# An attention block's transposes moved ahead of its value products, and a 96-row gate operand padded to 128 rows

## The chip, the core and the metric

The kernel runs on one core of a Trainium2 chip. Its time is device microseconds (us) of one execution, and what is compared is the median of several runs. The core has five engines with an instruction queue each: PE (TensorE, matrix products; PEld is its weight load), DVE (VectorE), ACT (ScalarE), POOL (GpSimd) and SP (SyncE, which here issues the DMA transfers). The order of each engine's instructions is fixed when the program is built, and an engine runs its own in that order, waiting wherever an operand or a buffer isn't ready.

## The reference: one step of a two-layer decoder

512 prompt tokens and 32 sample tokens (8 sequences of 4) go through an RWKV-7 layer and then a native sparse attention (NSA) layer, all in float32. Two places matter here.

The gate of the RWKV layer, whose low rank is 160:

```
g = jax.nn.sigmoid(xg @ g1) @ g2          # g1 (1024, 160), g2 (160, 1024)
```

and the attention of the NSA layer, which for each of 4 key heads `k` with 4 query heads each forms three softmaxes (compressed, selected and window keys), each times its values, and adds them with gates:

```
o_c = jnp.einsum('tkgn,nkd->tkgd', p_c.astype(v_cmp.dtype), v_cmp)
o_s = jnp.einsum('tkgjs,tkjsd->tkgd', p_s.astype(vg.dtype), vg)
o_w = jnp.einsum('tkgl,lkd->tkgd', p_w.astype(v_win.dtype), v_win)
o = g[..., 0:1] * o_c + g[..., 1:2] * o_s + g[..., 2:3] * o_w
```

With 512 prompt tokens the window and the selection hold all earlier tokens, so both are plain causal attention.

## The kernel before

`layer0` is the RWKV layer and `layer1` the NSA layer. Dense products are done in three passes of a split of each float32 operand into two `fp32r` parts (`products`, line 326, 128 x 128 weights against 272 tokens). Layer 1 has 28 such dense jobs (`dense`, in the order of `JO`), whose matmuls are mixed in between the attention's as filler: `together(attend(k), mix(jobs, sample), n)` takes `n` steps of the filler for each step of the attention.

Attention goes over key heads `k` = 0 to 3 and, in each, over four blocks `b` of 128 queries in the order `BO[k]`. `scores(k, b)` computes the score products (line 1733: 64 rows of contraction, 128 columns), adds the bias and takes the maximum on DVE (1740), the exponential on ACT (1743), and scales on DVE or POOL (1759). `values(k, b)` of one block runs beside `scores` of the next. It has 2(b+1) steps. Each step transposes the probabilities of four query heads into one PSUM bank (1777), copies them to an SBUF tile `h` on ACT (1780) or DVE (1782) in the pattern `aav`, and multiplies them with the values into `po`: line 1784, two column halves of 128 rows x 64 columns each (`PARS`), which write the lower and the upper 64 partitions. At the end the compressed branch is added into the same `po` (1789), `po` is copied out by ACT (1791), and it goes to DRAM, or in the last head to `gate` (1976) and `split`.

The sample tokens' attention (`attend_sample`) runs as filler as well: score products (1844, 128 rows x 32 columns), ten exponentials on ACT (1869), transposes (1885 to 1890), and value products (1918, 128 rows x 32 columns) on K and V rows that are loaded into tiles `s`. After the last head, `project_out` (326) and `project_last` (2009) multiply with the output weights; 2009 does tokens 256 to 511 (`h` = 1) first, then 0 to 255.

In this text a *form* of a matmul is its rows of contraction x columns of weights, rounded up to 32, 64 or 128: 1733 and 1693 are 64 x 128, 1784 and 1789 are 128 x 64, 1844 and 1918 are 128 x 32, and the dense jobs and the transposes are 128 x 128.

The buffers of layer 1 come from `M1`: 7 tiles `s` (sample rows, and at first the compression weights), 18 tiles `p` (K, V and queries), 6 tiles `h` (transposed probabilities and others). PSUM has 5 banks `pw` for the attention and 3 `ph` for the dense jobs.

In the gate of layer 0 (`gates`), the last 32 of the 160 hidden columns are stacked three times with their split parts into one operand of 96 rows (`gs`, `g2b`), so that one matmul does three products; line 361 (`stacked`) runs these beside the 128-row products. POOL writes rows 64 to 95 of `g2b` (685).

## Time and profile before

| | |
|---|---|
| median of 3 runs | 1086.18 us (1080.42 to 1086.69) |
| the profiled execution | 1075.55 us |
| its span, first to last instruction | 1073.8 us, mean granted TensorE clock 0.963 |
| PE busy | 990.1 us, 92% of the span |
| DVE, ACT, POOL busy | 621.1, 545.3, 454.0 us |
| attention of layer 1, first value transpose to the last | 692.7 to 1060.0 us |

A row of a group view gives the line, engine, operation, operands (`out<-in`, buffer numbers left out) and count, then busy time and mean duration, then the idle time just before these instructions and what ended it. In a timeline, the columns are the start in us, the duration, engine, line, operation and count of a merged run, and in brackets idle time with what ended it. In the view by windows each engine has its busy us, `(x...)` is its number of instructions, and `PEclk` is the granted TensorE clock as a share of full speed.

### The profile page before, as it was taken

The page shows a single profiled execution, that of the slowest core. Times are in us where ns is not written, and L with a number is a line of the kernel's source. Part 1 is how long each engine was busy: PE and PEld are TensorE (multiplying, and loading weights), DVE is VectorE, ACT ScalarE, POOL GpSimd, SP SyncE. Part 2 cuts the span into 40 slices and gives each one's busy share as a digit, 9 for nine tenths or more (in the row PEclk, how much of TensorE's full clock was granted, in tenths as well). Part 3 has the DMA queues.
Part 4 walks back from the last instruction along what each step waited for, and adds up shares of the span by engine and source line. Part 5 has one row for each costly group of instructions (what it writes and reads, how often), then busy time and mean ns, then how long its engine had stood idle before and what let it go on. Part 6 is the DMA issues. An engine that isn't in the chain of part 4 may idle for free.

```text
span 1073.8 us, 24587 instructions
## 1 busy us (share of the span) xinstructions
PE 990.1 (92%) x9525; PEld 838.6 (78%) x9525; DVE 621.1 (58%) x1390; ACT 545.3 (51%) x1254; POOL 454.0 (42%) x516
## 2 busy tenths in 40 slices
PE   5799998989999989999879799999899998998997
PEld 4789997978768678787778798986676774787876
DVE  4787679797666443468658234336555454327455
ACT  4456775646343354455445454456745646455352
POOL 5914647756620643213122757543224262145320
PEclk8799999999999999999989899999899996999999
DMA  5585435548472546635855533323242231327533
GB/s 187 189 277 192 136 118 155 191 154 262 121 209 74 170 129 190 194 96 146 192 177 169 166 110 107 95 79 115 70 136 76 70 105 41 105 84 263 152 114 104
DMA packets 149447, 153.54 MB, mean 143 GB/s; under 512 B 52946, under 2 KB 99570, under 8 KB 149074
## 3 DMA queue, kind: packets, MB, share of 16 engines
q1 hardware_dynamic: 149330, 151.97, 47.3%
q8 instruction: 75, 1.23, 0.5%
q14 instruction: 42, 0.34, 0.1%
HBM read 111.33 MB, written 43.93 MB: 145 GB/s over the span
## 4 chain that ended last, share of the span: by engine, by line
PE 53%; DVE 7%; DMA 6%; issue 4%; POOL 4%; ACT 3%; SPq 1%; DVEq 0%; POOLq 0%; ACTq 0%
PE ph L326 23%; PE pw L1733 5%; PE pw L1784 4%; PE pw L1777 4%; PE pr L1140 2%; DMA d<-dram 1%; PE ph L2009 1%; DMA w<-in_wo 1%; DVE l L288 1%; POOL l L288 1%; DMA tb<-dram 1%; DVE tmp L1042 1%; DVE p L721 1%; PE ph L1270 1%; PE pw L1789 1%
## 5 line engine op out<-in xcount | busy, mean ns | idle before, releaser
L326 PE MATMUL ph<-x,l 128*128 128x272 f32 x2448 | 359.4, 297 | 11.0 <-DVE l L288 3.3
L326 PEld LDWEIGHTS ph<-x,l 128*128 128x128 f32 x2448 | 322.5, 191 | 42.6 <-issue 20.8
L288 POOL TENSOR_TENSOR l<-w,l 128x512 fp32r<-128x512 f32 (+2 forms) x118 | 155.5, 1331 | 218.6 <-ACT l L287 202.2
L287 ACT ACTIVATE l<-w 128x512 fp32r<-128x512 f32 (+2 forms) x160 | 92.9, 613 | 149.7 <-PE ph L326 68.9
L326 PE MATMUL pp<-x,l 128*128 128x272 f32 x768 | 111.4, 299 | 5.9 <-POOL l L288 5.9
L326 PEld LDWEIGHTS pp<-x,l 128*128 128x128 f32 x768 | 103.7, 194 | 8.5 <-POOL l L288 6.2
L1743 ACT ACTIVATE a<-a,st 128x512 f32<-128x512 f32 (+3 forms) x128 | 70.6, 553 | 47.5 <-DVE st L1740 47.3
L1740 DVE CUSTOM_DVE_ANT_0 a<-pw,tb 128x512 f32<-128x512 f32 (+3 forms) x128 | 57.2, 487 | 58.0 <-PE pw L1733 57.6
L1733 PE MATMUL pw<-p,p 64*128 64x512 f32 (+3 forms) x256 | 65.0, 485 | 0.0
L1784 PE MATMUL pw<-h,p 128*64 128x256 f32 x320 | 52.4, 418 | 8.7 <-ACT h L1780 8.7
L1483 DVE TENSOR_TENSOR d<-ph,RS 128x272 f32<-128x272 f32 x56 | 24.3, 437 | 55.3 <-PE ph L326 50.9
L326 PE MATMUL pp<-t,l 128*128 128x272 f32 x384 | 54.2, 293 | 0.0
L1777 PE MATMUL pw<-cst,a 128*128 128x128 f32 x320 | 51.4, 292 | 1.5 <-DVE a L1759 1.5
L1777 PEld LDWEIGHTS pw<-cst,a 128*128 128x128 f32 x320 | 37.3, 147 | 19.4 <-issue 14.5
L1780 ACT ACTIVATE h<-pw 128x512 f32<-128x512 f32 x60 | 35.0, 590 | 32.5 <-PE pw L1777 32.1
L326 PEld LDWEIGHTS pp<-t,l 128*128 128x128 f32 x384 | 50.2, 188 | 0.7
L288 DVE TENSOR_TENSOR l<-w,l 128x512 fp32r<-128x512 f32 x42 | 36.5, 878 | 20.4 <-ACT l L287 20.2
L288 POOL TENSOR_TENSOR d<-d,d 128x544 fp32r<-128x544 f32 (+2 forms) x21 | 28.2, 1343 | 44.2 <-ACT d L287 35.4
L1759 DVE TENSOR_SCALAR a<-a,st 128x128 f32<-128x128 f32 (+3 forms) x112 | 43.4, 447 | 0.9
L1733 PEld LDWEIGHTS pw<-p,p 64*128 64x128 f32 x256 | 27.7, 193 | 18.4 <-issue 12.1
L1784 PEld LDWEIGHTS pw<-h,p 128*64 128x64 f32 x320 | 17.2, 139 | 26.3 <-ACT h L1780 11.0
L657 POOL TENSOR_TENSOR d<-d,d 128x544 f32<-128x544 f32 x8 | 10.8, 1346 | 56.4 <-ACT d L375 54.9
(415 smaller groups left out, 1937.9 us busy)
## 6 DMA issues: line engine op xcount, KB each, us to landing
w<-in_rkvz SPq DMA_DIRECT2D x64, 256.0 KB, 3.0
d<-dram SPq DMA_DIRECT2D x54, 272.0 KB, 4.2
w<-in_win SPq DMA_DIRECT2D x56, 256.0 KB, 3.0
dram<-d SPq DMA_DIRECT2D x48, 272.0 KB, 2.6
ab<-dram SPq DMA_DIRECT2D x32, 256.0 KB, 3.8
p<-in_xT SPq DMA_DIRECT2D x16, 272.0 KB, 3.8
tb<-dram SPq DMA_DIRECT2D x16, 264.0 KB, 4.9
dram<-uar SPq DMA_DIRECT2D x8, 512.0 KB, 3.7
```

The lines of the kernel that those rows point to most:

```text
L287: nc.scalar.activation(hi, raw, AF.Copy)
L288: (eng or nc.gpsimd).tensor_tensor(lo, raw, hi.bitcast(F32), OP.subtract)
L326: nc.tensor.matmul((pt[h][:m, :HN] if split else pt[:m, h, :HN]), a[:, k, :m], b[:, h * HN:(h + 1) * HN], start=(k == 0 and n == 0), stop= ...
L1140: nc.tensor.matmul(pg[par][r, i], BK[r, i, par], AR[r, i].rearrange("p a b -> p (a b)"), start=True, stop=True)
L1483: self.nc.vector.tensor_tensor(o, p, r, OP.mult)
L1733: nc.tensor.matmul(p[par][:, :n], Q[2 * k + m][r, tk], kk[par][r, :n], start=True, stop=True)
L1740: nc.vector.tensor_tensor_reduce(out=P[j], in0=p[par][:, :n], in1=tb, scale=-1.0, scalar=3.0e38, op0=OP.add, op1=OP.min, accum_out=st[:, 0 ...
L1743: nc.scalar.activation(P[j], P[j], AF.Exp, scale=-1.0, bias=st[:, 0, g, j:j + 1], accum_out=st[:, 1, g, j:j + 1])
L1759: (nc.gpsimd if e == "p" else nc.vector).tensor_scalar(pj, pj, rr, None, op0=OP.mult)
L1777: nc.tensor.transpose(pt[:, g % 2, g // 2], PB[g][j][:, c * 128:c * 128 + 128], ident)
L1780: nc.scalar.activation(w, pt, AF.Copy)
L1784: nc.tensor.matmul(po[r], v, w[:, par], start=(x == 0), stop=False, skip_group_check=True)
```

## The change

```diff
@@ PLAN
-    'M1': {'s': 7, 'p': 18, 'tb': 2, 'a': 12, 'h': 6, 'ct': 2, 'sc': 2},
+    'M1': {'s': 6, 'p': 13, 'tb': 2, 'a': 12, 'h': 12, 'ct': 2, 'sc': 2},
@@ gates, in layer 0
             gs = self.stack(self.t("p", dt=F32R), hid, 32)
             nc.scalar.activation(gs[64:96], hid[:32], AF.Copy)
+            nc.gpsimd.memset(gs[96:128].bitcast(F32), 0.0)
...
                 nc.gpsimd.tensor_tensor(g2b[64:96], raw[64:96], g2b[64:96].bitcast(F32), OP.subtract)
+                nc.gpsimd.memset(g2b[96:128].bitcast(F32), 0.0)
...
-                    self.stacked(pt, [(g2[0][:, c], gh), (g2[0][:, c], gl), (g2[1][:, c], gh), (g2b[:96, c], gs[:96])])
+                    self.stacked(pt, [(g2[0][:, c], gh), (g2[0][:, c], gl), (g2[1][:, c], gh), (g2b[:, c], gs)])
@@ values(k, b), in layer 1
             PB = self.PB[k, b]
-            po = self.t("pw", (128, 2, 128))
             steps = [(j, c, V[k][:, c]) for j, V in ((0, VS), (1, VW)) for c in range(b + 1)]
             ns = len(steps)
+            W = []
             for x, (j, c, v) in enumerate(steps):
...
-                for r, par in PARS:
-                    nc.tensor.matmul(po[r], v, w[:, par], start=(x == 0), stop=False, skip_group_check=True)
+                W.append(w)
                 for _ in range((4 * (x + 1)) // ns - (4 * x) // ns):
                     yield
+
+            po = self.t("pw", (128, 2, 128))
             for m in range(2):
                 for r, par in PARS:
-                    nc.tensor.matmul(po[r, m], VM[:, k, 2 * m + par], CT[k][:, b], start=False, stop=True, skip_group_check=True)
+                    nc.tensor.matmul(po[r, m], VM[:, k, 2 * m + par], CT[k][:, b], start=(m == 0), stop=False, skip_group_check=True)
+            for x, (j, c, v) in enumerate(steps):
+                for r, par in PARS:
+                    nc.tensor.matmul(po[r], v, W[x][:, par], start=False, stop=(x == ns - 1), skip_group_check=True)
             ok = self.t("h", (128, 2, 128))
```

The number of instructions of every kind stays the same but for three memsets on POOL. The order of the instructions that comes out of it moves. In the rows below a name like `pw_12648` is one buffer, and `x2` stands for two instructions of one row; lines after the change are 2 to 6 higher than before (transposes 1779 for 1777, value products 1795 for 1784, the compressed part 1792 for 1789, scores 1735 for 1733, copies 1782, 1784 and 1797 for 1780, 1782 and 1791, the sample's exponentials 1875 for 1869).

First place: PE, in the last head, where the value products of a block of eight steps stand (`po` is `pw_12648` before and `pw_12894` after). Before:

```order
L326 MATMUL ph_12695<-x_12251,l_12684 128x272
L1784 MATMUL pw_12648<-h_12663,p_10691 64x256 x2
L326 MATMUL ph_12695<-x_12250,l_12685 128x272
L326 MATMUL ph_12695<-x_12259,l_12684 128x272
L1784 MATMUL pw_12648<-h_12726,p_10691 64x256 x2
L1784 MATMUL pw_12648<-h_12735,p_10691 64x256 x2
L326 MATMUL ph_12695<-x_12260,l_12684 128x272
L326 MATMUL ph_12695<-x_12259,l_12685 128x272
L1733 MATMUL pw_12763<-p_9828,p_10985 128x384
```

After:

```order
L326 MATMUL ph_12880<-x_12244,l_12871 128x272
L1792 MATMUL pw_12894<-ct_12634,VM 64x128 x4
L1795 MATMUL pw_12894<-h_12656,p_10685 64x256 x2
L1795 MATMUL pw_12894<-h_12663,p_10685 64x256 x2
...
L1795 MATMUL pw_12894<-h_12851,p_10812 64x256 x2
L1735 MATMUL pw_12924<-p_9826,p_10906 128x128
```

Before, the block's products stand in seven places between dense matmuls; after, the compressed part and all eight steps stand in one run. Over layer 1, from the first score product on, consecutive matmuls on PE change their form 298 times before and 234 times after, and the products into `po` (1784, 1789) stand in 75 runs before and 31 after; up to that point both orders have the same number of changes.

Second place: PE, in the third head (`k` = 2), right behind the transposes of its compressed branch (1714). Before:

```order
L1733 MATMUL pw_11318<-p_10016,p_10234 128x384
L1777 MATMUL pw_11330<-cst,a_11018 128x128
L1777 MATMUL pw_11330<-cst,a_11057 128x128
L1777 MATMUL pw_11330<-cst,a_11118 128x128
L1777 MATMUL pw_11330<-cst,a_11155 128x128
L1784 MATMUL pw_11329<-h_11335,p_10691 64x256 x2
L1777 MATMUL pw_11339<-cst,a_11018 128x128
...
L1733 MATMUL pw_11451<-p_9827,p_10480 128x384
L1784 MATMUL pw_11329<-h_11344,p_10691 64x256 x2
L1733 MATMUL pw_11452<-p_9828,p_10480 128x384
```

After:

```order
L1735 MATMUL pw_11321<-p_10019,p_10232 128x384
L1779 MATMUL pw_11332<-cst,a_11021 128x128
...
L1779 MATMUL pw_11388<-cst,a_11151 128x128
L1735 MATMUL pw_11445<-p_9825,p_10472 128x384
...
L1735 MATMUL pw_11448<-p_10019,p_10472 128x384
L1779 MATMUL pw_11459<-cst,a_11022 128x128
...
L1779 MATMUL pw_11546<-cst,a_11152 128x128
L1792 MATMUL pw_11580<-ct_11315,VM 64x128 x4
```

Before, the first value product stands right behind the first four transposes. After, two runs of 16 transposes (four steps each) with four score products between them come ahead of the first value product. No dense matmul stands among these rows on either side; the next one follows after 36 rows before and after 66 rows now.

Third place: ACT, in the second head, where the sample's exponentials stand. Before:

```order
L1743 ACTIVATE a_9405,st_9291<-a_9405,st_9291 128x384
L1869 ACTIVATE s_9979,sst_10157<-s_9979,sst_10157 128x256
L1869 ACTIVATE s_10142,sst_10157<-s_10142,sst_10157 128x256
...
L1743 ACTIVATE a_9406,st_9291<-a_9406,st_9291 128x384
L1780 ACTIVATE h_9416<-pw_9411 128x512
```

After:

```order
L1745 ACTIVATE a_9452,st_9294<-a_9452,st_9294 128x384
L1782 ACTIVATE h_9416<-pw_9411 128x512
...
L1782 ACTIVATE h_9537<-pw_9532 128x512
L1875 ACTIVATE s_10153,sst_10157<-s_10153,sst_10157 128x120
...
L1875 ACTIVATE s_10153,sst_10157<-s_10153,sst_10157 128x32 x2
L1745 ACTIVATE a_9615,st_9513<-a_9615,st_9513 128x256 x2
L1782 ACTIVATE h_9625<-pw_9620 128x512
```

Before, eight of the ten exponentials stand ahead of the copy `h_9416` of the first transposed step in this stretch; after, all ten stand behind that copy and two more.

## The prediction

> **What bounds the kernel now.** I read the page from the top: busy shares, the 40 slices, the chain that ended last, then the groups.
>
> ```profile
> PE 990.1 (92%) x9525; PEld 838.6 (78%) x9525; DVE 621.1 (58%) x1390; ACT 545.3 (51%) x1254; POOL 454.0 (42%) x516
> ...
> PEclk8799999999999999999989899999899996999999
> ...
> PE 53%; DVE 7%; DMA 6%; issue 4%; POOL 4%; ACT 3%; SPq 1%; DVEq 0%; POOLq 0%; ACTq 0%
> ...
> L1784 PE MATMUL pw<-h,p 128*64 128x256 f32 x320 | 52.4, 418 | 8.7 <-ACT h L1780 8.7
> ```
>
> PE is busy for 92% of the span and carries over half of the chain; no other engine passes 58%. So time is won only by shortening what PE does, or by taking away one of its few waits. In layer 1 dense matmuls fill the attention's gaps, and the longest waits are the 8.7 us for the copies of 1780. The clock row has a 6 among its nines just there, in slice 34.
>
> A busy PE can still lose time between matmuls. The timeline of PE in the last head shows it, where nothing waits:
>
> ```profile
> 1014.19 1.53 PE L1777 MATMUL pw<-cst,a 128*128 128x128 f32 x12
> 1015.48 2.48 PE L326 MATMUL ph<-x,l 128*128 128x272 f32 x18
> ...
> 1027.46 0.65 PE L1784 MATMUL pw<-h,p 128*64 128x256 f32 x4
> 1028.04 1.52 PE L326 MATMUL ph<-x,l 128*128 128x272 f32 x10
> 1029.49 0.65 PE L1784 MATMUL pw<-h,p 128*64 128x256 f32 x4
> 1030.07 0.39 PE L326 MATMUL ph<-x,l 128*128 128x272 f32 x1
> 1030.39 1.08 PE L1784 MATMUL pw<-h,p 128*64 128x256 f32 x8
> 1031.41 1.27 PE L326 MATMUL ph<-x,l 128*128 128x272 f32 x8
> ```
>
> From start to start, one step's products (x4) hold PE for 0.58 us and two steps' (x8) for 1.02 us, so a step itself is worth 0.44 us, and 0.14 us is paid once per run. A dense run of one takes 0.32 us and one of ten 1.45 us: 0.126 us each, and 0.19 us once per run. Transposes next to dense matmuls, which have the same form, pay nothing of the kind: twelve in 1.29 us, 0.108 us each. So a change of form costs (0.14 + 0.19) / 2 = 0.165 us.
>
> **The change, part by part.**
>
> *Fewer changes of form.* In layer 1 the order has 298 changes before and 234 after, 64 fewer, each on the engine that bounds: 64 x 0.165 = 10.6 us. The saving is smaller than the 44 runs of value products that vanish would suggest (88 changes), since the sample's products (1918, a form of their own) are spread over more runs now. I take 10.5 us, with bounds of 8 (some changes stand beside waits) and 12 (0.19 for each).
>
> *The wait in the second head.* The timeline of PE, and the view by windows:
>
> ```profile
> 752.79 0.65 PE L1784 MATMUL pw<-h,p 128*64 128x256 f32 x4 [2.21 <-ACT h L1780]
> ...
> 755.06 0.33 PE L1777 MATMUL pw<-cst,a 128*128 128x128 f32 x1 [1.18 <-DVE a L1759]
> 755.72 0.48 PE L1777 MATMUL pw<-cst,a 128*128 128x128 f32 x1 [0.33 <-DVE a L1759]
> 757.31 1.12 PE L1784 MATMUL pw<-h,p 128*64 128x256 f32 x4 [1.12 <-ACT h L1780]
> ```
> ```profile
> 755.00:760.00 5.00, 3.49 (x14) 2.19 (x14) 2.98 (x15) 2.74 (x11) 1.56 (x3) 0.56 0.09 26
> 760.00:765.00 5.00, 5.00 (x31) 2.96 (x30) 2.16 (x9) 2.27 (x9) 1.53 (x4) 0.76 0.04 5
> ```
>
> PE stands for 4.84 us in four pieces, and behind that the granted clock is 0.56 and 0.76 over ten microseconds: 5 x 0.44 + 5 x 0.24 = 3.4 us lost, some 0.7 of it while PE stood anyway. Together 7.5 us. The reason is on ACT, where the sample's exponentials run ahead of the copy (here in the third head, the same ten):
>
> ```profile
> 887.81 0.38 ACT L1869 ACTIVATE s<-s,sst 128x120 f32<-128x120 f32 x1
> ...
> 888.19 0.49 ACT L1869 ACTIVATE s<-s,sst 128x256 f32<-128x256 f32 x1
> ...
> 888.68 0.49 ACT L1869 ACTIVATE s<-s,sst 128x256 f32<-128x256 f32 x1
> ...
> 889.17 0.31 ACT L1869 ACTIVATE s<-s,sst 128x32 f32<-128x32 f32 x1
> ...
> 889.47 0.31 ACT L1869 ACTIVATE s<-s,sst 128x32 f32<-128x32 f32 x1
> ```
>
> Start to start they take 0.38 (120 wide), 0.49 (256) and 0.30 us (32); two, four and four of them make 3.9 us. In the new order three copies go ahead of all ten. The first product that needs a copy from behind them comes on PE only after 12 dense matmuls (1.5 us), 22 transposes (2.4), the eight score products and eight value products, some 7 us altogether, against 3.9 us of exponentials and two exponentials of scores. So most of the wait is covered. Waits of the 1759 kind can come back, since the blocks still follow each other. I take 5 us gained; bounds 0 and 7.5.
>
> *The wait in the third head.*
>
> ```profile
> 892.96 1.12 PE L1784 MATMUL pw<-h,p 128*64 128x256 f32 x4 [4.63 <-ACT h L1780]
> 894.02 2.82 PE L1777 MATMUL pw<-cst,a 128*128 128x128 f32 x12
> ```
> ```profile
> 890.00:895.00 5.00, 2.04 (x9) 1.28 (x10) 0.76 (x5) 5.00 (x20) 0.00 (x0) 0.71 0.17 53
> 895.00:900.00 5.00, 5.00 (x16) 2.73 (x15) 3.28 (x10) 2.62 (x6) 3.51 (x4) 0.50 0.16 58
> 900.00:905.00 5.00, 5.00 (x13) 1.44 (x12) 1.04 (x4) 0.69 (x3) 0.91 (x3) 0.50 0.19 53
> 905.00:910.00 5.00, 5.00 (x23) 3.84 (x23) 1.08 (x5) 2.49 (x8) 0.00 (x0) 0.58 0.00 0
> ```
>
> Here 4.63 us of standing are followed by a halved clock that lasts, though PE is busy: 5 x (0.29 + 0.50 + 0.50 + 0.42) = 8.5 us lost, about 8.1 without the part that PE stood. Together 12.7 us. The new order doesn't move the exponentials here: the same eight stand ahead of the first copy. But 16 transposes no longer wait behind a value product. They need PSUM banks: one is free, since `po` isn't held yet, and DVE gives back the four of the scores half a microsecond apart. So PE does 12 transposes more (1.3 us) before it must wait for ACT, and the wait breaks into pieces, some 3 to 3.5 us in all. Whether the clock then falls is open. If it doesn't, 9 us are gained; if it does, the stretch without dense matmuls is longer now (66 rows against 36), perhaps 6 to 7 us are lost to it, and 2.5 us are gained. I take 5; bounds +2 (a longer halving) and -9.
>
> *The end.* The last 48 dense products of 2009 wait for the last block's output:
>
> ```profile
> 1063.34 6.63 PE L2009 MATMUL ph<-x,l 128*128 128x272 f32 x48 [1.15 <-ACT x L287]
> ```
>
> Now twelve products of the other half of the tokens (12 x 0.126 = 1.5 us) stand between the last value product and these. The 1.15 us goes.
>
> *The padded gate.*
>
> ```profile
> 399.51 1.15 PE L361 MATMUL ph<-p,p 96*128 96x272 f32 x7 [0.64 <-POOL p L685]
> ...
> 437.82 0.77 PE L361 MATMUL ph<-p,p 96*128 96x272 f32 x4
> 438.52 0.76 PE L1140 MATMUL pr<-ab,ab 64*64 64x128 f32 x5
> ```
> ```profile
> L1063 POOL MEMSET q<- 128x512 f32 x8 | 4.2, 528 | 0.0
> ```
>
> Four matmuls of 96 rows alone take 0.70 us, as 0.19 + 4 x 0.126 = 0.69 would have it for 128 rows. Padding gives PE nothing. [...] The three new memsets are priced by the nearest one, 0.53 us. Two of them stand on POOL right ahead of 685, for which PE already waits 0.64 us once: 0 to 1.1 us more, I take 0.5.
>
> *Fewer buffers.* `s` goes from 7 to 6, `p` from 18 to 13, so some loads wait longer for a release, and what is queued behind them on SP waits too.
>
> ```profile
> SPq L297 <- POOL l L288: 88.5, 26, 13.3
> ...
> PE ph L1918 <- DMA s<-in_wvn: 0.7, 2, 0.4
> ```
>
> From 690 to 1000 us SP already waits for buffers of weights up to 13.3 us at a time, and PE waits for a sample load only twice, 0.7 us in all: the loads run ahead. I take 1 us; bounds 0 and, with ten more runs of 1918 waiting 0.4 us each, 4 us.
>
> **Sum.** -10.5 - 5 - 5 - 1.1 + 0.5 + 1 = -20 us, against the profiled execution's 1075.55 us (span 1073.8). The three timed runs lie 5 to 11 us above it, and nothing in the page says why; I put the difference on their median: 1086.2 - 20 = 1066 us. A measurement of this kernel tells about 1% from no change, here 1075.3 us.
>
> **The rivals.**
>
> *Only the changes of form count.* The exponentials hold up ACT all the same, the waits move but stay: -10.5 - 1.1 + 1.5 = -10, 1076 us. For it: in the third head the ACT order is the same. Against it: in the second head it isn't.
>
> *Both dips of the clock go.* No wait is long enough any more: -10.5 - 7.5 - 9 - 1.1 + 0.5 = -27.6, 1058.5 us. For it: single waits get shorter in both places. Against it: the clock fell behind a single 2.2 us wait with small ones around it, too.
>
> *Slower: the sample's rows come too late.* With six `s` tiles, and four of them held by compression weights until the last compression, each load of K and V rows is issued only when PE has finished with the tile before, and lands later than PE gets there.
>
> ```profile
> s<-in_csk SPq DMA_DIRECT2D x32, 64.0 KB, 1.9
> s<-in_wvn SPq DMA_DIRECT2D x8, 256.0 KB, 4.1
> ```
>
> One exposed load costs 2 to 4 us and, with the clock halved for a stretch as above (3.4 us), about 6. It decides from five on: 30 - 20 = +10, and with six 1102 us. Against it stand the 0.7 us of before with one tile more.
>
> *No gain: the clock falls in every long stretch of attention.* The stretch at 895 to 905 us ran at 0.50 although PE was busy throughout, with transposes and small forms; the change makes such stretches purer. With +5 in place of -5 in the third head, +1 in place of -5 in the second, and half a 3.4 us window in two others: -10.5 + 5 + 1 + 3.4 - 1.1 + 1.5 = -1, 1085.5 us. [...] Against it, the row at 1014.19 us: twelve transposes ran at full pace there, after dense work; and the longest run of them now is 16 x 0.108 = 1.7 us.
>
> **How the numbers follow.** Forecast 0.43, both dips gone 0.19, only the changes 0.23, no gain 0.07, slower 0.08. Faster by over 1%: nearly all of the first (0.42), the second, and 0.09 of the third, whose 1076 us lies on the bound: 0.70. Within 1%: 0.22. Slower: 0.08. The likeliest case alone spans 1058 to 1074 us. The range leaves out the lower tail of the second case and, above, the last two: 1051 to 1083 us.
>
> **What would show it.** Right: the busy time of 1795 falls from 52.4 us for 320, since fewer of them start a run; the dense group's mean of 297 ns falls slightly; the wait by 752 us is gone, that by 893 us is in pieces; twelve of 2015 stand before the last 48 without a gap; 96 or 128 rows in 361 make no difference. Wrong: waits of 1850 or 1918's successor for DMA above 5 us in sum; a clock below 0.7 in more slices than before; or the same count of short runs on PE at the same total.

## The result, and the profile after

The changed kernel took 1046.5 us in the median of four runs (1044.3 to 1061.7) and the kernel before, run beside it, 1083.3 us (1072.3 to 1086.7): a ratio of 0.968, 95% interval 0.960 to 0.976, 36.8 us less. The forecast was 20 us less, 1066 us, and the measured time lies 4.5 us below the lower end of the range.

Two later comparisons, on two chips, gave less: 0.979 (0.973 to 0.984) and 0.976 (0.972 to 0.981). The cause is in the list of runs, where each has its mean granted clock. A straight line through 96 runs of the kernel before, on six chips (1066 to 1090 us), falls by 9.0 us for each 0.01 of clock and leaves a scatter of 2.6 us; at 0.963, the clock of the profile that the prediction used, it gives 1074.1 us. With the same slope three sets of the changed kernel come to 1053.1, 1052.2 and 1050.4 us at 0.963, weighted 1051.8: **22.3 us less at the same clock**. Part of the rest is clock. Over all runs it is 0.960 before and 0.965 after (17 runs, mean 1049.9 us, before 1076.7), which is worth 4.4 us; what is left of the 36.8 us, some 10 us, is which runs happened to meet in the first comparison. Three of its four changed runs had a clock of 0.969 to 0.972; the clocks of its timed runs of the kernel before aren't on record, so this last part is argued from the line. Below, "at 0.963" means this line.

The first profile of the changed kernel was of a disturbed execution (clock 0.954), so the lines here are from a second profile of the same kernel (span 1050.6 us, clock 0.964). Its page:

```profile
PE 982.3 (93%) x9525; PEld 847.5 (81%) x9525; DVE 617.2 (59%) x1390; ACT 543.3 (52%) x1254; POOL 455.1 (43%) x519
...
PEclk8799999999999989889999999999989999999999
...
L326 PE MATMUL ph<-x,l 128*128 128x272 f32 x2448 | 357.1, 298 | 10.7 <-ACT l L287 3.2
...
L1795 PE MATMUL pw<-h,p 128*64 128x256 f32 x320 | 41.9, 394 | 0.2 <-ACT h L1782 0.2
```

The value products fell from 52.4 to 41.9 us of busy time, and the idle time before them from 8.7 to 0.2 us. The dense group, 297 ns a piece before, has 298. The waits of PE from 630 us on, longest sums first (the list before began with the 8.7 us for the copies of 1780):

```profile
PE ph L326 <- DVE x L288: 2.2, 2, 1.9
PE pw L1735 <- ACT h L1782: 0.7, 1, 0.7
...
PE pw L1795 <- ACT h L1782: 0.2, 1, 0.2
```

The timeline of PE in the second head, where it stood for 4.84 us:

```profile
752.26 1.53 PE L1779 MATMUL pw<-cst,a 128*128 128x128 f32 x12
753.72 0.66 PE L1792 MATMUL pw<-ct,VM 128*64 128x128 f32 x8
754.21 1.46 PE L1795 MATMUL pw<-h,p 128*64 128x256 f32 x12
755.60 0.72 PE L1735 MATMUL pw<-p,p 64*128 64x128 f32 x8
756.52 0.65 PE L1795 MATMUL pw<-h,p 128*64 128x256 f32 x4 [0.20 <-ACT h L1782]
```

And in the third, where it stood for 4.63 us, with the view by windows (PE, PEld, DVE, ACT, POOL, then the clock):

```profile
883.25 1.40 PE L1735 MATMUL pw<-p,p 64*128 64x384 f32 x4
884.81 0.91 PE L1735 MATMUL pw<-p,p 64*128 64x384 f32 x2 [0.17 <-DVE st L1742]
886.41 0.91 PE L1735 MATMUL pw<-p,p 64*128 64x384 f32 x2 [0.69 <-ACT h L1782]
887.25 1.96 PE L1779 MATMUL pw<-cst,a 128*128 128x128 f32 x16
889.14 0.66 PE L1792 MATMUL pw<-ct,VM 128*64 128x128 f32 x8
889.63 1.90 PE L1795 MATMUL pw<-h,p 128*64 128x256 f32 x16
```
```profile
885.00:890.00 5.00, 4.31 (x32) 2.91 (x33) 3.37 (x13) 5.00 (x18) 0.00 (x0) 1.00 0.02 5
890.00:895.00 5.00, 5.00 (x41) 2.94 (x36) 3.81 (x16) 4.83 (x15) 3.56 (x6) 1.00 0.01 2
895.00:900.00 5.00, 5.00 (x41) 4.42 (x42) 3.60 (x14) 2.46 (x9) 1.05 (x1) 1.00 0.23 82
```

ACT is as full there as before, but PE stands behind it for 0.69 us only, and the clock stays at 1.00. At the end the twelve products and the last 48 are one run of 60, with no wait:

```profile
1037.19 1.95 PE L1795 MATMUL pw<-h,p 128*64 128x256 f32 x16
1039.06 7.75 PE L2015 MATMUL ph<-x,l 128*128 128x272 f32 x60
```

**Where the time went.** The trace of the kernel before gives the clock as 1.00 or 0.50, in 26 windows of 3.41 to 170.7 us that are multiples of 3.41 us but for the last, which is cut off. Four passes of 1784 took 0.65 us at full clock (1027.46 us) and 1.12 us at half clock (892.96 us). If half of the time at half clock is taken off a stretch, profiles can be laid side by side matmul by matmul (both have 9525). In us of full clock, before and after:

| stretch | before | after |
|---|---|---|
| start to the gate's first product (361) | 379.1 | 380.1 |
| from there to the first score product of layer 1 | 229.5 | 223.8 |
| from there to the last matmul | 421.8 | 405.0 |
| ... of it, PE idle | 16.5 | 5.9 |
| ... matmuls at the pace of the middle of a run | 351.6 | 351.6 |
| ... what is left: starts and ends of runs | 53.2 | 47.5 |

Layer 1 gives 16.8 us, 10.6 of them waits; some 5 us come from layer 0. (The idle row is in plain us. In the column before, the three parts come to 421.3 us, so 0.5 us of it is left unassigned.) The "pace of the middle" is the mean distance of matmuls of one kind that stand among others of the same form. What is left depends on which matmuls count as the middle; the differences between the columns hardly do. By the form of the run, before and after: value products 11.2 and 5.1 us (75 and 31 runs), dense and transposes 20.6 and 16.8 (119 and 95), sample products 6.9 and 8.4 (34 and 44), and the 64-row scores 14.3 and 16.9 us, though they stand in 63 runs now instead of 69. The last is the surprise of this table.

### The profile page after: what moved, and what is told of

It reads as the page before. It is cut to its first block, busy times and chain, and to the rows that moved or that the text cites. A ratio compares the mean times of both kernels' runs of the same rounds, so it can differ in the third digit from the quotient of the medians.

```text
span 1059.9 us, 24576 instructions
## 1 busy us (share of the span) xinstructions
PE 990.7 (93%) x9525; PEld 855.2 (81%) x9525; DVE 617.4 (58%) x1390; ACT 543.1 (51%) x1254; POOL 455.3 (43%) x519
## 5 line engine op out<-in xcount | busy, mean ns | idle before, releaser
L1745 ACT ACTIVATE a<-a,st 128x512 f32<-128x512 f32 (+3 forms) x128 | 70.7, 554 | 27.6 <-DVE st L1742 27.5
L1485 DVE TENSOR_TENSOR d<-ph,RS 128x272 f32<-128x272 f32 x56 | 24.4, 437 | 74.4 <-PE ph L326 74.2
L1735 PE MATMUL pw<-p,p 64*128 64x512 f32 (+3 forms) x256 | 61.8, 461 | 1.3 <-ACT h L1782 0.7
L326 PE MATMUL pp<-t,l 128*128 128x272 f32 x384 | 57.8, 305 | 0.0
L326 PEld LDWEIGHTS pp<-t,l 128*128 128x128 f32 x384 | 53.6, 200 | 0.8
L1779 PE MATMUL pw<-cst,a 128*128 128x128 f32 x320 | 48.5, 285 | 0.0
L1795 PE MATMUL pw<-h,p 128*64 128x256 f32 x320 | 42.3, 396 | 0.7 <-ACT h L1782 0.7
L1761 DVE TENSOR_SCALAR a<-a,st 128x128 f32<-128x128 f32 (+3 forms) x112 | 39.9, 416 | 0.9
L1761 POOL TENSOR_SCALAR a<-a,st 128x512 f32<-128x512 f32 x16 | 26.7, 1675 | 30.9 <-PE pw L1779 16.7
L1142 PE MATMUL pr<-ab,ab 64*64 64x128 f32 x256 | 34.6, 286 | 2.2 <-ACT q L1136 2.2
```

Source lines behind the costliest of these rows:

```text
L326: nc.tensor.matmul((pt[h][:m, :HN] if split else pt[:m, h, :HN]), a[:, k, :m], b[:, h * HN:(h + 1) * HN], start=(k == 0 and n == 0), stop= ...
L1142: nc.tensor.matmul(pg[par][r, i], BK[r, i, par], AR[r, i].rearrange("p a b -> p (a b)"), start=True, stop=True)
L1485: self.nc.vector.tensor_tensor(o, p, r, OP.mult)
L1735: nc.tensor.matmul(p[par][:, :n], Q[2 * k + m][r, tk], kk[par][r, :n], start=True, stop=True)
L1745: nc.scalar.activation(P[j], P[j], AF.Exp, scale=-1.0, bias=st[:, 0, g, j:j + 1], accum_out=st[:, 1, g, j:j + 1])
L1761: (nc.gpsimd if e == "p" else nc.vector).tensor_scalar(pj, pj, rr, None, op0=OP.mult)
```

## The experiments

My theory (A in the expectations): fewer changes of form, and waits behind copies that go. The rivals: the waits alone (B), the padding (C), the clock (D, E).

| kernel | median, us (runs) | at 0.963 | PE idle in layer 1 |
|---|---|---|---|
| before | 1076.0 (96) | 1074.1 | 16.5 |
| the change | 1049.4 (17) | 1051.8 | 5.9 |
| the order and buffers, no padding | 1059.8 (6) | 1058.5 | 5.5 |
| the buffers alone | 1080.0 (12) | 1073.9 | 13.1 |
| the padding alone, two sets | 1068.1, 1068.2 (12, 12) | 1066.4, 1066.3 | 14.9, 15.3 |
| the memsets alone | 1069.3 (12) | 1067.7 | 14.7 |
| products two steps late | 1061.6 (6) | 1062.1 | 9.4 |
| `po` taken early | 1049.1 (6) | 1053.3 | 6.9 |

The standard error of a value at 0.963 is 0.3 us in the first row and 0.6 to 1.2 us in the others.

**The change without the padding.** The edit, against the changed kernel:

```diff
-            nc.gpsimd.memset(gs[96:128].bitcast(F32), 0.0)
-                nc.gpsimd.memset(g2b[96:128].bitcast(F32), 0.0)
-    ... (g2b[:, c], gs)])
+    ... (g2b[:96, c], gs[:96])])
```

> The change without the padding of the gate's operand (96 rows stay 96): the new order of the value products and the new buffer counts alone. PE has 299 runs of one form of matmul from the first attention product on in the kernel before, 235 in the changed kernel and 232 here. Theory A (fewer changes of form at 0.165 us each, about 10.5 us, and the rest of the gain from waits and from the clock's dips behind them in layer 1): as fast as the changed kernel, 1044 to 1052 us, 31 to 39 us under the kernel before. Theory C (a good part of the gain is the padding, in layer 0, where the prediction gave it nothing): 5 to 15 us slower than the changed kernel, 1052 to 1062 us, with layer 0's segment (start to layer 1's first matmul of the square input) as long as before's, 398 us. Theory B (the waits alone, form changes hidden): the same as A here.

1058.5 us at 0.963: 15.6 us less than before, 6.7 more than the change. C holds for part of the gain.

**The buffers alone.**

```diff
-    'M1': {'s': 7, 'p': 18, 'tb': 2, 'a': 12, 'h': 6, 'ct': 2, 'sc': 2},
+    'M1': {'s': 6, 'p': 13, 'tb': 2, 'a': 12, 'h': 12, 'ct': 2, 'sc': 2},
```

> The kernel before with the new buffer counts alone (h 12, p 13, s 6), old order of the value products, no padding; 306 runs of one form, where the kernel before has 299. Theory A: the value products still wait each for its own copy, and the forms change as often, so -5 to +4 us against before (1078 to 1088 us): the waits at 752 and 888 us of the kernel before come from a product behind a copy that h 12 doesn't bring earlier. Theory B (a buffer of h that came free late made the copies, and so the products, late): most of the waits go, 1058 to 1072 us, with only the change of order left out. Theory C: the same as A, within 3 us of before.

No difference (-0.2 us at 0.963). The first two rows of the waits in its layer 1:

```profile
PE pw L1784 <- ACT h L1780: 8.6, 4, 4.6
PE ph L2009 <- ACT x L287: 1.2, 1, 1.2
```

The wait for copies is what it was, 8.6 us for 8.7. So it was the place of the products, not a buffer that came free late; and fewer `s` and `p` cost no time that shows, though one wait of 1.0 us for a load of sample rows (`s<-in_wk`) is new.

**The padding alone, twice, and the memsets alone.**

```diff
+            nc.gpsimd.memset(gs[96:128].bitcast(F32), 0.0)
+                nc.gpsimd.memset(g2b[96:128].bitcast(F32), 0.0)
-    ... (g2b[:96, c], gs[:96])])
+    ... (g2b[:, c], gs)])
```

The last two lines are left out in the kernel with the memsets alone.

> The kernel before with the padding of the gate's operand alone (two memsets, 128 rows in place of 96 in the fourth product); 295 runs of one form, before 299. Theories A and B: within 3 us of before (+0.5 us for the memsets, 0 to -0.7 for four fewer changes of form): 1081 to 1088 us, and the fourth product of a gate tile takes the same time with 96 and 128 rows. Theory C (the padding is worth part of the gain): 5 to 15 us faster than before, 1068 to 1078 us, with the gain ahead of layer 1's first square product.

> The padding alone once more (as the third experiment), for a second profile and on another set of runs: before 1074.8 us and the padding 1066.4 us at a clock of 0.963, so 6 to 10 us faster if that was the kernel; 0 to 3 us faster if it was that set of runs. In the profile the 128-row products of the gate follow each other without the wait of 0.8 us (full-clock time from the gate's first product to its 300th matmul: 16.8 us, before 19.6 us).

> The kernel before with the two memsets on POOL alone: they write rows 96 to 127 of the gate's operands, but the product still uses 96 rows. The order of PE's instructions in layer 0 moves nearly as with the padding. Theory P1 (the padding's gain comes from the moved order in layer 0, by which a 96-row product no longer stands waiting 0.8 us with others behind it, and not from the 128 rows): as fast as the padding alone, 1064 to 1071 us, 6 to 10 us under before. Theory P2 (the 96-row product itself costs PE time): as slow as before, 1073 to 1080 us.

Against my forecast of nothing, the padding is worth 7.8 us, in both sets. The memsets alone give 6.5 us, with 96 rows still in the product. The gate's first products in the timeline of the padding alone, and below it of the memsets alone:

```profile
399.03 1.77 PE L361 MATMUL ph<-p,p 128*128 128x272 f32 x12
...
403.09 0.77 PE L361 MATMUL ph<-p,p 128*128 128x272 f32 x4
...
404.91 2.26 PE L361 MATMUL ph<-p,p 128*128 128x272 f32 x16
```
```profile
398.75 1.77 PE L361 MATMUL ph<-p,p 128*128 128x272 f32 x12
...
402.81 0.77 PE L361 MATMUL ph<-p,p 96*128 96x272 f32 x4
...
404.63 2.28 PE L361 MATMUL ph<-p,p 128*128 128x272 f32 x16
```

The four products take 0.77 us with 96 rows and with 128: the rows cost nothing here. But with the memsets the order of the whole layer comes out another way. The first 32 of these products stand in three pieces instead of four, and none waits for line 685, for which PE stood 0.64 us before. From the gate's first product to its 32nd, over the same 191 matmuls in every kernel, it is 7.9 us of full clock in the sixteen profiles of kernels with memsets and 8.8 us in the four without; to the 64th (723 matmuls) it is 45.1 to 47.0 and 47.3 to 48.9 us. (The 16.8 and 19.6 us to the 300th matmul, in the expectation above, aren't over the same matmuls: 36 dense ones with the padding, 41 before.) From the gate's first product to layer 1, three kernels without memsets took 226.4 to 230.3 us and seven with them 221.0 to 226.8, some 5 us less in the mean. The nine other profiles with memsets spread wider, 222.0 to 230.0, and the fourth without took 239.4, so the size is loose; 1 to 3 us more come in layer 1, whose order the memsets move as well (294 changes of form, 298 before).

**Products two steps late.** A kernel between both orders: each value product follows its transposes by two steps and not by none, and not all in one run.

```diff
+            def product(x):
+                for r, par in PARS:
+                    nc.tensor.matmul(po[r], steps[x][2], W[x][:, par], start=(x == 0), stop=False, skip_group_check=True)
             for x, (j, c, v) in enumerate(steps):
...
                 W.append(w)
+                if x >= 2:
+                    product(x - 2)
...
+            for x in range(max(ns - 2, 0), ns):
+                product(x)
```

> The changed kernel, with its buffers and its padding, but each value product issued two steps behind its own transposes, between the transposes of the later steps, and not in one run at the end: each product has two steps of transposes (some 0.9 us of PE) between its copy's start and itself, and the forms change nearly as often as before (296 runs of one form, before 299, the changed kernel 235). Theory A (form changes cost 0.165 us each, waits and dips the rest): the waits of the second and third head go, the form changes stay, so 10 us slower than the changed kernel, 1054 to 1062 us. Theory B (only the waits behind the copies count, form changes lie hidden): as fast as the changed kernel, 1043 to 1050 us. Theory D (the length of the run in one form matters for the clock, so that short runs bring its dips): no faster than before by more than 8 us, 1073 to 1084 us, with as many slices at half clock in layer 1 as before has.

1062.1 us at 0.963, as theory A had it: 10.3 us more than the change, and 4.3 less than the padding alone, which has the old order of products. Its idle time in layer 1 is 9.4 us: the wait of the second head is gone, and one of 3.6 us is left in the third.

**The bank.** `po` is taken at the start of a block's values, as before:

```diff
             PB = self.PB[k, b]
+            po = self.t("pw", (128, 2, 128))
...
-            po = self.t("pw", (128, 2, 128))
```

> The changed kernel, but the output bank po is taken at the start of a block's values, as in the kernel before, so that four of the five pw banks are left to the transposes and the scores while it is held; the order of the products and the number of changes of form (235) are those of the changed kernel. Theory F1 (the order gains by fewer changes of form and by each product's copy being long done): as the changed kernel within 3 us. Theory F2 (a good part of what is beyond the changes of form comes from the bank that is free for the transposes): 4 to 9 us slower than the changed kernel, with waits of L1779 for a bank's release by ACT or DVE.

1053.3 us at 0.963, the changed kernel within the scatter. F2 falls: the fifth bank is worth nothing here.

**The clock.** The changed kernel, unaltered, twice more:

> The changed kernel, unaltered, on the same chip as the three below and with more runs of the kernel before beside it. Its first comparison gave -36.8 us, but its undisturbed runs there had a granted clock of 0.969 to 0.972, and those of the kernel before on the chip of the first four experiments 0.949 to 0.971. A straight line through those 23 runs (time against clock) falls by 8.9 us for each 0.01 of clock, and at 0.963 it gives 1074.8 us for before, 1058.5 for the order alone, 1066.4 for the padding alone and 1053.1 for the changed kernel. Theory E1 (the first comparison was flattered by the clock of its runs; the change itself doesn't move the clock): 1050 to 1057 us at a mean clock as before's within 0.003, that is 19 to 25 us faster. Theory E2 (the change itself keeps the clock up, since the waits that led to half-clock windows are gone): 1042 to 1049 us, mean clock 0.967 or more where before has 0.961, 28 to 37 us faster.

> The changed kernel a third time, for its clock: so far the mean granted clock of 46 runs of the kernel before is 0.9605, of 11 runs of the changed kernel 0.965, of 6 with the bank taken early 0.968. If the change itself keeps the clock up, 0.964 to 0.969 here with before at 0.958 to 0.963, and 1046 to 1052 us; if the first comparison was flattered by its runs' clock alone, a mean clock within 0.002 of before's and 1052 to 1056 us.

Mean clocks of 0.964 and 0.965, and of 0.960 and 0.959 for before beside them. Neither theory is whole: most of the first comparison's surplus was its runs, and some 0.005 of clock seems to belong to the change. Over the kernels of this study the clock goes with the idle time in layer 1, though not strictly: 0.965 with 6 us, 0.960 with 16.5, 0.957 with 46, 0.947 with 66 and 0.931 with 74, but 0.9685 with 11 (the last four are score kernels below), and 0.962 with 5.5 in the order without padding. The traces show more than this row. Layer 1 of all twenty profiles, up to its last products, can be cut into the steps of 3.41 us in which the clock changes. Where PE stood for over 60% of a step at full clock, the next step was at half clock in 32 of 32 cases; where it stood for 40 to 60%, in 25 of 41; where it stood for less than 5%, in 13 of 1983. These 13 all came behind a step that the compressed scores (1693 before, 64 rows and a stream of 32 columns) filled by over 60%, which happened 16 times. So in these profiles a dip came behind every step in which PE stood for over 60%, and behind 13 of 16 steps that these small products filled, with PE counted as busy; steps in which PE stood for 5 to 40% aren't in these counts.

Layer 1's time at half clock is 18.3 to 28.1 us (mean 24.4) in the five profiles with the old order of products and the old scores, and 11.4 to 25.4 us (mean 16.2) in six with the new order, which is worth 4 us and fits the 4.4 us of the mean clock. Ahead of layer 1 it is 44 to 72 us in the twenty profiles, and nothing here tells what sets it there; in the eleven it hides the difference, since the six had 6 us more at half clock there.

**The price of a change of form by itself.** Work that no output uses is added behind the last product: 256 transposes and 64 value products (in the trace each of their two halves is two passes, 256 passes in all), once mixed and once in long runs.

```diff
+            for _ in range(64):            # the other kernel: 8
+                for n in range(4):         # 32
+                    nc.tensor.transpose(pt[:, n % 2, n // 2 % 2], x[:, 0, 0:128], ident)
+                for n in range(1):         # 8
+                    for r, par in PARS:
+                        nc.tensor.matmul(po[r], x[:, par, 0:64], x[:, 0, 0:256], start=True, stop=True)
```

> The changed kernel with work added at its end, which no output uses: 64 times four transposes (128 x 128) and then one value product's two halves (128 x 64), in that order on PE, 127 changes of form. Against the next kernel, with the same matmuls in 16 runs (15 changes), it measures the price of a change by itself. At 0.165 us (the prediction's price) it ends 18.5 us later than the next one; at 0.10 us (what is left of the order's gain in the traces when the long waits are taken off: 6 us for 61 to 64 changes) 11 us later; if the transposes hide it, 0 to 3 us.

> The same added work as in the kernel ahead, which no output uses, but in 8 times 32 transposes and then 16 halves of value products: 15 changes of form. From the durations in the traces, 256 transposes of 0.108 us and 64 value products of 0.44 us make 27.6 + 28.2 = 56 us, so 1108 us at a clock of 0.963, with the added stretch between 56 and 60 us.

The timeline of the first, and of the second:

```profile
1116.47 0.65 PE L2024 MATMUL pw<-d 128*64 128x256 f32 x4
1117.06 0.66 PE L2021 MATMUL pw<-cst,d 128*128 128x128 f32 x4
1117.64 0.65 PE L2024 MATMUL pw<-d 128*64 128x256 f32 x4
```
```profile
1090.69 3.67 PE L2024 MATMUL pw<-d 128*64 128x256 f32 x32
1094.30 3.71 PE L2021 MATMUL pw<-cst,d 128*128 128x128 f32 x32
1097.94 3.67 PE L2024 MATMUL pw<-d 128*64 128x256 f32 x32
```

A pair of runs takes 1.17 us from start to start in the first and 7.25 us for eight times the work in the second. Between the starts of the first and the last added matmul lie 73.96 and 57.61 us, both at full clock, with 121 and 15 changes of form: 16.35 / 106 = **0.154 us for a change**. Over their runs the two kernels are 17.1 us apart at 0.963 (1127.0 and 1110.0 us), with an error of 2.0. The prediction's 0.165 was nearly right, for this pair of forms; the changes to 64 rows or 32 columns weren't priced by themselves.

At 0.154 us for each run of one form, the table's runs should have given 6.8 us at the value products (44 fewer), 3.7 at dense and transposes (24 fewer) and 0.9 at the scores (6 fewer), and taken 1.5 at the sample products (10 more): 9.9 us for the net 64. They gave 6.1, 3.8, -2.6 and -1.5 us. So three of the four came nearly as priced, and what is missing is at the scores, 3.5 us.

**Fewer runs of sample products.**

```diff
                         VV.append(v)
-                        yield
```

> The changed kernel, with the pause taken away that lets other work in between two loads of the sample tokens' value rows: their products stand in 15 runs on PE and not in 24, and the changes of form fall from 235 to 225. At 0.10 to 0.165 us each 1 to 1.7 us faster than the changed kernel, so 1050 to 1052 us at a clock of 0.963 (the changed kernel 1052.7); if the rows now come late, a wait of several us stands before these products and it is slower than the changed kernel.

1049.7 us at 0.963, 2.1 less than the change with an error of 1.7: as expected in size, but not told apart from nothing. The other outcome came in part as well: PE now waits 2.3 us in all, 1.7 us at most, for a load of sample rows (`s<-in_csv`).

**Score products side by side.** In the trace of the kernel before two score products on different halves of the rows start 6 or 7 ns apart. The timeline of the changed kernel shows what happened where the order tore such a pair apart:

```profile
743.94 1.13 PE L1735 MATMUL pw<-p,p 64*128 64x256 f32 x8
...
749.70 1.13 PE L1735 MATMUL pw<-p,p 64*128 64x256 f32 x4
750.75 0.52 PE L326 MATMUL ph<-x,l 128*128 128x272 f32 x2
751.20 1.13 PE L1735 MATMUL pw<-p,p 64*128 64x256 f32 x4
```

Eight passes took 1.13 us where both halves worked side by side, and four took 1.13 us where a dense run had come between and each run worked on one half only, all at a granted clock of 1.00. Each of a pair has its own bank here, and as soon as one is free its product can be ordered alone. Passes that started without a partner within 20 ns: 84 of 256 before, 96 after. Three kernels hold pairs together as a unit of the scheduler, two on the changed kernel (fours, twos), one on the kernel before, and a fourth adds the edit of the sample runs:

```diff
+                with self.tc.tile_critical():
                     for p, kk in ((pa, KA[k]), (pb, KW[k])):
+                    # twos: the unit stands here, around one p
                         for r, par in PARS:
```

> The changed kernel, with the four score products of a pair of query heads (rows 0 to 63 and 64 to 127 in turn) issued on PE as one unit, so that nothing comes between them: they stand in 31 runs instead of 52, and the changes of form fall from 235 to 191. In the traces two score products on different halves of the rows start 7 ns apart and take 0.52 us together (512 columns), while two on the same half, or one by itself, take 0.53 us each; of 256 score passes before 84 stood alone, in the changed kernel 96, and the time that score runs take beyond the paired pace grew from 14.4 to 17.0 us. Theory S (half of the expected saving by fewer changes of form went into score products torn apart): 5 to 12 us faster than the changed kernel, 1040 to 1047 us at a clock of 0.963, unless waiting for the fourth bank costs more. Rival W (a unit has to wait for all its banks, and PE stands for them): no faster than the changed kernel, 1050 to 1062 us, with long waits of the score line for DVE.

> The changed kernel, with each two score products (one on rows 0 to 63, one on 64 to 127) issued as one unit: every pair runs side by side, but a unit needs only two banks; 56 runs of score products, 230 changes of form. Theory S: nearly all of the 5 to 8 us that pairing alone is worth, 1044 to 1048 us at 0.963. If the gain of the one in fours is the number of changes instead, about the changed kernel's 1052 us.

> The kernel before with the scores in fours alone: 263 changes of form instead of 299, every pair of score products side by side. Theory S: 5 to 12 us under the kernel before, 1062 to 1069 us at 0.963; the waits at 752 and 888 us stay.

> The kernel with the scores in fours and without the pause between two loads of the sample's value rows: 184 changes of form, sample products in 14 runs. 0 to 2 us faster than the scores in fours alone, by 7 changes of 0.15 us.

1075.8, 1118.2, 1113.2 and 1079.5 us at 0.963 (the second ran at 0.931, outside the 0.946 to 0.971 of the line's runs). All are slower than the kernel that they were made from; the last is 3.7 us over the fours alone, where 0 to 2 us less were expected. Rival W is right, and had put the loss too low: PE stood for 45.7, 74.3 and 65.9 us in layer 1 in the first three, while only 0, 6 and 0 of the 256 passes started without a partner. From the waits of the fours:

```profile
PE pw L1736 <- ACT s L1876: 5.3, 1, 5.3
...
PE pw L1736 <- DMA out_kv<-KD: 4.1, 1, 4.1
...
PE pw L1736 <- POOL l L288: 3.1, 2, 2.6
```

Such a unit waited here for work that the scores don't use, a store of K (4.1 us) and the split of a dense weight (3.1 us). So these times say nothing of pairs. But the score time on PE without waits, at full clock, does: 56.1 us before, 57.2 in the changed kernel, 42.8 in fours, 50.2 in twos. (The expectation below has 41.5 and 44.1; these take off waits at half clock as if they were at full clock.) So with nearly every pair whole, twos save 7 us, and what the fours save beyond that may come of their fewer runs. A pair can also be held by its buffer:

```diff
-                pa = [self.t("pw", (128, 512)) for _ in range(2)]
...
+                    if j == 0 or b > 1:
+                        pq = self.t("pq", (128, 2, 512))
...
+                        nc.tensor.matmul(pq[:, par, o2:o2 + n], Q[2 * k + m][r, tk], kk[par][r, :n], start=True, stop=True)
...
-    k.open(ctx, space=PSUM, pw=PLAN["PW1"], ph=8 - PLAN["PW1"])
+    k.open(ctx, space=PSUM, pw=3, pq=1, ph=3)
```

> The changed kernel, but the score products of two query heads on different halves of the rows write into the two banks of one PSUM tile, which is taken as a whole, so that both can go side by side without a unit that waits for everything; the scores have this one tile and the attention's other work three banks, where all shared five. 251 changes of form (the changed kernel 235), since the two kinds of keys of the long blocks come one after the other. Score products took 56.1 us of PE in the kernel before, 57.2 in the changed one, 41.5 and 44.1 in the kernels with fours and twos. Theory S (score products torn apart cost 13 us in both kernels): score time 44 to 46 us, 13 us less, 2.4 us more for 16 changes of form, and 0 to 6 us of waits for the fewer banks: 1041 to 1047 us at a clock of 0.963, where the changed kernel has 1052. Rival W (the banks bound): 1052 us or more, with waits of the transposes or of the scores for DVE or ACT of over 10 us.

1050.5 us at 0.963, 1.3 less than the change, where I had expected 5 to 11. Scores and compressed scores fell from 69.4 to 59.5 us of PE (the scores alone from 57.2 to 50.9, where 44 to 46 were expected), 26 passes still start without a partner, and fours of 256 columns now read

```profile
745.68 0.70 PE L1740 MATMUL pq<-p,p 64*128 64x256 f32 x4
```

but idle time rose from 5.9 to 11.3 us, and dense and transposes pay 2.9 us more for their runs. Some of the idle time stands at the end of the last head, where the dense filler had run out:

```profile
1024.16 1.12 PE L1783 MATMUL pw<-cst,a 128*128 128x128 f32 x6 [2.67 <-DVE a L1765]
1025.70 1.04 PE L1783 MATMUL pw<-cst,a 128*128 128x128 f32 x4 [0.42 <-ACT h L1786]
...
1031.45 6.62 PE L2019 MATMUL ph<-x,l 128*128 128x272 f32 x48 [1.16 <-ACT x L287]
```

A last kernel gives the filler out more slowly there:

```diff
-    'N': (3, 4, 4, 4),
+    'N': (3, 4, 4, 3),
```

> The kernel whose score products share a tile, with three steps of filler for each step of the attention in the last head, where there were four. In that kernel's last head the dense filler ends 11 us before the last value products, and then PE waits 2.67 us for DVE (the scaling of the scores), 0.42 us for a copy and 1.16 us for the last block's output, with only attention left. With filler left over for these places: 2 to 4 us faster than with four steps, 1046 to 1049 us at a clock of 0.963 (1050.6 before), and the three waits under 1.5 us together. If the scores are the chain there and not the filler, the waits only move and the time is the same within 1.5 us.

The end of its last head:

```profile
1013.82 2.52 PE L2019 MATMUL ph<-x,l 128*128 128x272 f32 x18
1017.33 1.12 PE L1783 MATMUL pw<-cst,a 128*128 128x128 f32 x6 [0.99 <-DVE a L1765]
1018.87 0.66 PE L1783 MATMUL pw<-cst,a 128*128 128x128 f32 x4 [0.43 <-ACT h L1786]
...
1024.67 6.55 PE L2019 MATMUL ph<-x,l 128*128 128x272 f32 x48 [1.15 <-ACT x L287]
```

The wait of 2.67 us is 0.99 now; the three sum to 2.6 us, more than the 1.5 expected. 1047.1 us at 0.963 and 1045.3 in the median (1036.8 to 1048.8, ratio to before 0.972, 0.967 to 0.976): 4.7 us under the change at the same clock, with an error of 1.4. It is the fastest kernel of the study by that measure.

## Why the prediction missed, point by point

- **The basis failed.** "The three timed runs lie 5 to 11 us above it, and nothing in the page says why; I put the difference on their median" is the step. It took three runs whose clock was unknown for the kernel's time, and a difference forecast from one profile for the difference between two sets of runs. Runs of the kernel before lie between 1066 and 1090 us with the clock, and the mean clock of the changed kernel is higher by 0.005. Put on the profiled execution, whose clock is close to the mean, the same sum gives 1055.5 us, and 1051.8 was measured at that clock; the range, moved along, would be 1040 to 1072 us and hold the 1046.5.
- **That 20 is near 22.3 is luck.** The single terms were off by more than the sum was: the changes of form gave 4.8 us less than forecast, the padding 7 us more, the buffers 1 us more.
- **The padding failed.** Forecast +0.5, measured -7.8 alone and -6.7 on top of the order. The row was read rightly, four products took 0.77 us with 96 rows and with 128. What I left out is that three more instructions on POOL move the order of the program far beyond the gate. The two orders have the same number of changes of form ahead of the attention, and I took that for no difference.
- **Changes of form, mis-sized:** forecast -10.5, came -5.7. The price was right for the pair of forms that was measured (0.154 for 0.165), and so was the number, 64, which already holds the ten more runs of sample products. The scores failed: six fewer runs of them should have given 0.9 us, and they cost 2.6 us more. More of their passes stand without a partner (96 for 84), which a price per change leaves out. That this is the whole of it isn't shown; in the kernel with the shared tile, where 26 passes stand without a partner, the scores took 50.9 us for 57.2.
- **The waits and the end: the size right, the parts not.** Forecast 5 + 5 + 1.1 = 11.1 us with the clock's dips behind the waits, and PE stands 10.6 us less without any dip counted. All of the 1.15 us and nearly all of the 4.84 and 4.63 us went; I had expected 3 to 3.5 us of pieces in the third head, and 0.9 us stayed. The dips were priced from one execution. In five profiles with the old order a dip stands behind both waits, but in the third head it lasts 17 us in the one that I read and 3.4 us in the other four. With the new order, three of six profiles have none there, and in the second head five of six still have one, some 10 us later and behind a busy PE. So the clock is better priced as a mean over runs, 9.0 us for 0.01.
- **Fewer buffers:** forecast +1, measured -0.2 with an error of 0.8.
- **The rivals.** "Both dips go" has nearly the right size, 27.6 us for 26.8 over all runs, for another reason: the third head's dip went in half of the profiles, and in the second head one still came, behind the compressed scores. "No gain" falls: transposes and small forms ran at 1.00 from 885 to 900 us, and runs of 32 transposes, 3.71 us each, did so at the end of the grouped kernel. A busy PE did lose the clock here, but behind compressed scores (13 of 16 steps). "Sample rows late" falls: no wait for a sample load is left.
- **The signs.** The group of 1795, both heads, the end and the gate's products came as written; the dense mean didn't fall.

Summed with what was measured: layer 1 -16.8, layer 0 about -5, the mean clock -4.4, together -26.2 us, for 26.8 between the means of all runs. Open is what in layer 0, beyond the 1 us up to the gate's 32nd product, gives the rest, since stretches there differ by up to 4 us between profiles of one kernel, and what sets the clock ahead of layer 1.

## What to carry to other kernels

Ask for the granted clock of the runs before a difference is put on their median, and compare at one clock: 0.01 of it went with 9.0 us here. Where a scheduler orders the program, a memset can be worth more than the edit it belongs to (two of them gave 6.5 us here, and the 128 rows took the 0.77 us that 96 took): read the new order of every stage, not only of the one that was meant. And look for pairs of small matmuls that run side by side: the order can tear them apart at no visible wait (96 of 256 passes stood without a partner in the changed kernel), and a shared output tile held most of them together here (26 stood without) at 1050.5 us, where the changed kernel with atomic units took 1075.8 and 1118.2 us (all at 0.963).

## What the runs showed of the hardware

- Two matmuls on rows 0 to 63 and 64 to 127 side by side: four passes of 256 columns took 0.70 us from the first start to the last end (the kernel with the shared tile, 745.68 us), torn apart 1.13 us (the changed kernel, 749.70 us).
- A change of form between 128 x 128 and 128 x 64 cost 0.154 us of PE (16.35 us for 106 changes between the two kernels with added work), though PE counts as busy over it.
- 96 and 128 rows of contraction took the same, four products in 0.77 us (the memsets alone and the padding alone).
- Runs of the kernel before, each on one core, spread over 24 us on six chips and over 21 us on one of them; a line in the granted clock, 9.0 us for 0.01, takes up four fifths of the variance of the 96.
- In the twenty profiles, in layer 1, the clock fell to half in 32 of 32 steps of 3.41 us behind one in which PE stood for over 60%, and in 13 of 16 behind one that products of 64 rows and 32 streamed columns filled by over 60%, with PE busy; behind the 1967 other steps with PE busy for over 95% it never fell.
